# A hybrid four-layer model on one Trainium2 core: in the recurrent layer, other copies ahead of the triangular inverse, value rows moved by transfers, and two narrow products left whole

## The chip, the cores and the metric

The kernel runs on 1 core of one Trainium2 chip. The metric is the device time of one launch in microseconds (us). The kernel before was run three times: 2401.36, 2402.68 and 2403.2 us, median 2402.68 us. The profile is of one further execution.

## The reference, cut to what matters

Four layers, each a mixer and a gated feed-forward part, over 512 tokens of width 1024 in float32. The change lies in the first mixer alone, an RWKV-7 recurrence with 16 heads of 64:

```python
xx = token_shift(x) - x
xr, xw, xk, xv, xa, xg = (x + xx * mu[c] for c in range(6))
r, k, v = einsum('cbsd,cde->cbse', stack([xr, xk, xv]), w_rkv)
w = -softplus(-(w0 + tanh(xw @ w1) @ w2)) - 0.5      # w1: 1024 x 64
a = sigmoid(a0 + (xa @ a1) @ a2)                     # a1: 1024 x 64
g = sigmoid(xg @ g1) @ g2
kk = hs(k * k_k)
kk = kk * rsqrt(maximum(sum(kk * kk, -1), 1e-24))    # a sum over each head
k = k * (1 + (a - 1) * k_a)
def step(state, r_t, d_t, k_t, v_t, kk_t, a_t):      # 512 steps, state 64 x 64 per head
    sa = einsum('bhvk,bhk->bhv', state, kk_t)
    state = state * d_t - sa * (kk_t * a_t) + v_t * k_t
    return state, einsum('bhvk,bhk->bhv', state, r_t)
```

After it come the group norm of the outcome, the gate and the product with w_o.

## The kernel before, in words

**How the work is ordered.** The program records every operation, and a scheduler of its own writes each engine's order before the build (`Program.run`). All recorded operations therefore carry line 239 in the profile, and groups are told apart by tile names. The generators of the recurrence are interleaved by strings of letters and digits (`FIRST`, `PAIRED`, `ORDERS`, lines 28 to 34); the scheduler then moves operations within a window. Where it foresees that TensorE (PE) would stand idle it adds products of the identity (`keep_warm`, line 525), called fills here.

**Full products** split each float32 operand into a rounded part and the rest, both float32r, and take three float32r products for one (`mm3`). A split costs a cast on ScalarE (ACT) and a subtraction on VectorE (DVE): tiles `slot` for activations, `whi` and `wlo` for weights, read from `wraw`.

**The recurrent mixer** (`rwkv`, line 1009) works in these steps.
1. The k projection, then `heads`: the sum of squares of each head, by a product of the squared rows `t` with a 0/1 matrix of 16 columns (`selr`), 8 row tiles in split halves, so 16 products.
2. The r projection in 8 blocks of 24 products. Between them stand three narrow products (`lora`): w1 and a1 with 64 columns each (48 products in all, in split halves), and g1 with 128. `mixed` blends a row tile with its shifted one (DVE, tile `t`) and splits it. The results of w1 and a1 are the two halves of `twa`.
3. The v projection (`values`, tiles `v`), interleaved by `FIRST` with `ahead` (decays and scaled keys of a group of four heads, `rwkv_prepare`) and with the first `solve`.
4. For each of four groups of four heads, `solve`: `rwkv_products` masks 64-token blocks of key products into the tile `pr` or `pa`; `rwkv_inverse` inverts their triangles; `rwkv_direct` applies the inverses to the keys. The inverse first brings the 16x16 blocks on the diagonals together: eight ACT copies of 32 rows and 256 elements into `zx` (tiles `slot` or `et`), one DVE transpose, one addition. Then a loop of 15 steps on DVE, two operations a step, a second transpose, and two levels of products (`invert`, tiles `mt`, `low`, `iv`), whose two halves alternate by `PAIRED`.
5. `rwkv_chain` (line 1416) runs through the 8 chunks of 64 tokens of a group in turn, two chunks to a block b. Each chunk takes the state `st`, makes `vu` and makes the next state. A `vu` tile has 64 rows of v, copied from `v` by ACT (`vu<-v`, line 1445), and 64 rows of results from PSUM (`vu<-ps`); the pool holds four such tiles, two blocks. `ORDERS[n]` interleaves the chain of group n (c) with the outcome `rwkv_out` (o) and with the `solve` of group n+1 (p).
6. `rwkv_out_proj` multiplies by w_o (`et,rk`) beside the last chains, and the feed-forward part follows.

The few lines of `rwkv_inverse` that the change replaces:

```python
for k in range(4):
    r, o = slice(k * 32, k * 32 + 32), k % 2 * 32 + (P if k < 2 else 64)
    nc.scalar.copy(turn(zx4[r, :, 0, :]), turn(z3[r, o:o + 16, :]))
    nc.scalar.activation(turn(zx4[r, :, 1, :]), turn(z3[r, o + 16:o + 32, :]), AF.Identity, scale=mk['odd'][r])
nc.vector.transpose(n, zx)
nc.vector.tensor_add(n1, n2[:, :, 0, :], n2[:, :, 1, :])
```

Of the kernel before, what the change touches and what calls it, by code (L numbers as in the profile page):

```python
# [17 lines left out]
P = 128  # L18
S = 512
D = 1024  # L20
KT = D // P
HID = 2816
HT = HID // P
NB = S // P
# [482 lines left out]
class K:  # L507
# [509 lines left out]
    def rwkv(self, g, g_next, slots):  # L1017
# [5 lines left out]
        nc, d = self.nc, self.d  # L1023
# [6 lines left out]
        lp = self.pool("lp", 2, inner)  # L1030
        keep, sel, selr, rs = one("keep"), one("sel", w=46), one("selr", F32R, 30), one("kkrs", w=NB * 16)
        self.weight_pools(2, 2, wide, side="right")
# [10 lines left out]
        nc.vector.memset(sel[64:, 15:16], 1.0)  # L1043
        nc.vector.tensor_copy(selr, sel[:, :30])
        near, rbc = self.rstd(ms)
        xx = []

        def mixed(c, k):
            t = tp.tile([P, S], F32, name="t")
            x = xp.tile([P, S], F32R, name="slot"), xp.tile([P, S], F32R, name="slot")  # L1050
            nc.vector.scalar_tensor_tensor(t, xx[k], v['rw_mu'](c * KT + k), hn[k], op0=ALU.mult, op1=ALU.add)
            self.split(t, *x)
# [32 lines left out]
        for n in range(KT):  # L1085
            sq = tp.tile([P, S], F32, name="t")
            nc.scalar.activation(sq, kf[n], AF.Square, scale=v['rw_k_k'](n))
            part = [xp.tile([P, S], F32R, name="slot") for _ in range(2)]
            self.split(sq, *part)
            for j, t in enumerate(part):  # L1090
                nc.tensor.matmul(heads[:16], selr[:, 14 - 2 * n:30 - 2 * n], t, start=n + j == 0, stop=n == KT - 1 and j == 1)
        x = [mixed(0, k) for k in range(KT)]
        for n in range(KT):
            self.gemm(d['rw_w_r'][n], x, lambda ps: nc.scalar.copy(rf[n], ps))
            if n == 1:
                hs = tp.tile([P, S], F32, name="t")
                nc.scalar.copy(hs[:16], heads[:16])
                ps = self.bank()
                for b in range(NB):
                    nc.tensor.transpose(ps[:, b * 16:(b + 1) * 16], hs[:16, b * P:(b + 1) * P], self.ident[:16, :16])  # L1100
                hc = self.sm.tile([P, NB * 16], F32, name="kkss")
                nc.vector.tensor_scalar(hc, ps[:, :NB * 16], 1e-24, None, op0=ALU.max)
# [10 lines left out]
        cp = self.pool("cp", 1, early)  # L1113
        mk = cp.tile([P, 7 * 64 + 1], F32, name="mk")
        nc.sync.dma_start(mk, d['rw_masks'])
# [118 lines left out]
    def rwkv_prepare(self, sb, rf, kf, twa, keep, sel, rs, ka1):  # L1234
# [18 lines left out]
        for i, p in enumerate(sb['pairs']):  # L1253
# [13 lines left out]
            nc.scalar.activation(ei, sw, AF.Exp, scale=DEC)  # L1267
            nc.scalar.copy(wide.rearrange("p (b h d) -> p b h d", b=NB, h=2), rs3[:, :, 2 * p:2 * p + 2].unsqueeze(3).to_broadcast([P, NB, 2, 64]))
            nc.vector.tensor_copy(pend[:, i, :], self.blocks(e, NC)[:, :, C - 1])
# [45 lines left out]
    def rwkv_inverse(self, sb):  # L1315
# [4 lines left out]
        col = lambda j: slice(j * P, (j + 1) * P)  # L1320
        zx = self.part("et")
        zx4 = zx.rearrange("p (t x u) -> p t x u", t=16, x=2)
        z = sb['pr']
        z3 = z.rearrange("p (u t) -> p t u", u=16)
        for k in range(4):
            r, o = slice(k * 32, k * 32 + 32), k % 2 * 32 + (P if k < 2 else 64)
            turn = lambda t: t.rearrange("p t u -> p u t")
            nc.scalar.copy(turn(zx4[r, :, 0, :]), turn(z3[r, o:o + 16, :]))
            nc.scalar.activation(turn(zx4[r, :, 1, :]), turn(z3[r, o + 16:o + 32, :]), AF.Identity, scale=mk['odd'][r])
        n, tt, tmp = self.part("et"), self.part("et"), self.part("et")  # L1330
        nc.sync.dma_start(tt, self.d['rw_eye'])
        nc.vector.transpose(n, zx)
        n2, t4 = n.rearrange("p (t b m) -> p t b m", t=16, b=2), tt.rearrange("p (j b i) -> p b j i", j=16, b=2)
        n1 = zx[:, :256].rearrange("p (t m) -> p t m", t=16)
        nc.vector.tensor_add(n1, n2[:, :, 0, :], n2[:, :, 1, :])
        for i in range(1, 16):
# [69 lines left out]
    def rwkv_chain(self, sb, tg):  # L1406
# [11 lines left out]
        for b in range(NB):  # L1418
# [21 lines left out]
            for c, (rv, ru) in enumerate(halves):  # L1440
# [556 lines left out]
def consts():  # L1997
    import numpy as np
    i = np.arange(P)
    freq = (10000.0 ** (-2.0 * (i % 32) / 64)).astype(np.float32).reshape(P, 1)  # L2000
    s, t = i[:, None], i[None, :]
    s6, t6 = s % 64, t % 64
    even, odd = np.where(t < 64, s6 <= t6, s6 < t6), np.where(t < 64, s6 < t6, s6 <= t6)
    c = t[:, :64]
    low = [(s6 // (2 * m) == c // (2 * m)) & (s6 % (2 * m) >= m) & (c % (2 * m) < m) for m in (16, 32)]
    masks = [even, odd] + low + [s6 // 16 == c // 16, (s % 32 >= 16)]
# [19 lines left out]
def arrays(inputs):  # L2026
# [32 lines left out]
    a['rw_w_r'], a['rw_w_k'], a['rw_w_v'] = groups(rkv[0]), np.ascontiguousarray(rkv[1]), np.ascontiguousarray(rkv[2])  # L2059
    for n, m in (('rw_w1', 64), ('rw_a1', 64), ('rw_g1', P)):  # L2060
        a[n] = groups(a[n][0], m)[0]
    a['sw_w_qkv'] = groups(a['sw_w_qkv'][0])
# [77 lines left out]
```

## Time and profile before

| | |
|---|---|
| Three runs | 2401.36 to 2403.2 us, median 2402.68 us |
| Profiled execution | 2403.21 us, of which the span is 2401.4 us |
| Share of the span busy | PE 98%, DVE 81%, ACT 60%, POOL 14% |
| Recurrent mixer | from the start to some 420 us |
| Mean granted clock of PE | 0.997 of full speed |

How to read it: times inside the span count from its start. Two engines' work lies side by side, so a saving counts only where that engine is what the others wait for. PE's matmuls overlap each other in the records: one shown with 0.39 us can follow the last after 0.23 us, so PE's pace is taken from starts, not from durations. A float32 product stands as two records, a float32r one as one. "ACT" in the chain of waits means that the step was held by an ACT operation. In this kernel PE loads weights under PEld.

### The profile page before, as it was taken

What the parts mean: (1) busy time and instruction counts of PE and PEld (TensorE: products, weight loads), DVE (VectorE), ACT (ScalarE), POOL (GpSimd) and SP (SyncE); (2) the same over time, 40 slices, a digit from 0 to 9 for tenths busy, and PEclk for the clock granted to TensorE, in tenths of its full rate; (3) what the DMA queues carried; (4) which work ended last, traced back from release to release, by engine and by line L of the source; (5) the groups of instructions that cost most, each with busy time, mean ns of one, the idle gap of its engine ahead of it and who ended that gap; (6) DMA issues with size and microseconds to landing.
All of it is one profiled execution on the core that took longest, in us unless ns stands there. A gap on an engine that the chain in (4) does not pass through costs nothing.

```text
span 2401.4 us, 37056 instructions
## 1 busy us (share of the span) xinstructions
PE 2356.2 (98%) x13692; PEld 1939.1 (81%) x13692; DVE 1944.5 (81%) x3280; ACT 1450.9 (60%) x2540; POOL 328.1 (14%) x398
## 2 busy tenths in 40 slices
PE   9999889999999999999999999999999999999998
PEld 8577779988888768888887888888888778988886
DVE  8778986886879787868699888886869978886868
ACT  4666765755556587555575444755557747755555
POOL 0000000221121001211211100121111101121110
PEclk9999999999999999999999999999999999999999
DMA  4220012899998326999988754899898757899985
GB/s 160 84 77 13 9 66 72 193 209 229 219 212 206 89 72 140 212 230 227 212 216 208 196 152 104 183 217 222 220 219 207 171 138 168 203 204 232 219 209 117
DMA packets 129285, 404.27 MB, mean 168 GB/s; under 512 B 14416, under 2 KB 21072, under 8 KB 129104
## 3 DMA queue, kind: packets, MB, share of 16 engines
q0 software_dynamic: 51840, 176.18, 40.9%
q1 hardware_dynamic: 77264, 225.72, 28.1%
q8 instruction: 108, 1.77, 0.3%
q14 instruction: 73, 0.60, 0.1%
HBM read 397.39 MB, written 2.10 MB: 166 GB/s over the span
## 4 chain that ended last, share of the span: by engine, by line
PE 79%; DVE 7%; ACT 6%; DMA 4%; issue 4%; POOL 0%; SPq 0%; DVEq 0%; ACTq 0%; POOLq 0%
PE ps L239 78%; DMA wraw<-ffn_w_b 3%; DVE slot L239 2%; ACT slot L239 2%; DVE wlo L239 2%; ACT whi L239 1%; ACT et L239 1%; DMA wraw<-ffn_w_a 1%; DMA wraw<-ffn_o_b 0%; ACT vu L239 0%; DVE left L239 0%; DMA wraw<-sg_w_o 0%; ACT wu L239 0%; ACT L239 0%; DVE h L239 0%
## 5 line engine op out<-in xcount | busy, mean ns | idle before, releaser
L239 PE MATMUL ps<-whi,slot 128*128 128x512 f32 (+1 forms) x5072 | 1553.9, 384 | 4.8 <-DVE slot L239 4.2
L239 PEld LDWEIGHTS ps<-whi,slot 128*128 128x128 f32 x5072 | 943.5, 188 | 179.9 <-ACT whi L239 9.1
L239 ACT CAST whi<-wraw 128x1024 fp32r<-128x1024 f32 (+3 forms) x845 | 689.4, 836 | 563.1 <-PE ps L239 437.7
L239 DVE TENSOR_TENSOR wlo<-wraw,whi 128x1024 fp32r<-128x1024 f32 (+3 forms) x845 | 792.9, 955 | 244.9 <-ACT whi L239 243.3
L239 PE MATMUL ps<-wlo,slot 128*128 128x512 f32 (+1 forms) x2536 | 969.2, 383 | 3.1 <-DVE wlo L239 3.1
L239 PEld LDWEIGHTS ps<-wlo,slot 128*128 128x128 f32 x2536 | 476.6, 188 | 87.6 <-DVE wlo L239 7.4
L239 PE MATMUL ps<-slot,whi 128*128 128x512 f32 (+1 forms) x720 | 229.8, 396 | 2.0 <-ACT slot L239 1.3
L239 DVE TENSOR_TENSOR slot<-ps,slot 128x512 f32<-128x512 f32 (+2 forms) x271 | 161.3, 609 | 47.1 <-PE ps L239 32.9
L239 ACT CAST slot<-left 128x512 fp32r<-128x512 f32 (+1 forms) x294 | 164.8, 590 | 53.3 <-PE ps L239 29.4
L239 DVE TENSOR_TENSOR slot<-left,slot 128x512 fp32r<-128x512 f32 (+1 forms) x294 | 184.0, 647 | 11.0 <-ACT slot L239 6.9
L239 DVE TENSOR_TENSOR h<-h,ps 128x512 f32<-128x512 f32 x240 | 160.0, 685 | 27.9 <-PE ps L239 25.2
L239 POOL DMA_DIRECT2D wraw<-ffn_w_a x128 | 110.0, 863 | 500.5 <-DVE wlo L239 404.6
L239 PEld LDWEIGHTS ps<-slot,whi 128*128 128x128 f32 (+1 forms) x720 | 131.7, 186 | 40.0 <-DVE slot L239 7.9
L239 PE MATMUL ps<-slot,wlo 128*128 128x512 f32 (+1 forms) x360 | 140.3, 392 | 0.4 <-DVE wlo L239 0.4
L239 POOL DMA_DIRECT2D wraw<-ffn_w_b x64 | 55.0, 867 | 423.0 <-DVE wlo L239 156.3
L239 ACT COPY slot<-ps 128x512 f32<-128x512 f32 (+1 forms) x144 | 78.6, 563 | 36.7 <-PE ps L239 34.5
L239 POOL DMA_DIRECT2D wraw<-ffn_o_a x64 | 54.7, 855 | 285.3 <-DVE wlo L239 157.4
L239 ACT COPY left<-ps 128x512 f32<-128x512 f32 x108 | 54.9, 558 | 57.2 <-PE ps L239 57.2
L239 PE MATMUL ps<-ident,slot 128*128 128x128 f32 x561 | 86.2, 277 | 1.3 <-ACT slot L239 0.6
L239 PEld LDWEIGHTS ps<-ident,slot 128*128 128x128 f32 x561 | 63.3, 141 | 26.6 <-DVE slot L239 12.1
L239 PEld LDWEIGHTS ps<-slot,wlo 128*128 128x128 f32 (+1 forms) x360 | 66.7, 185 | 15.2 <-DVE wlo L239 1.2
L239 DVE SCALAR_TENSOR_TENSOR slot<-slot,ncol 128x512 f32<-128x512 f32 (+1 forms) x96 | 65.1, 702 | 9.2 <-ACT slot L239 9.0
(301 smaller groups left out, 2095.5 us busy)
## 6 DMA issues: line engine op xcount, KB each, us to landing
wraw<-ffn_w_a SPq DMA_DIRECT2D x128, 512.0 KB, 6.8
wraw<-ffn_w_a POOLq DMA_DIRECT2D x128, 512.0 KB, 7.0
wraw<-ffn_o_a SPq DMA_DIRECT2D x64, 512.0 KB, 5.1
wraw<-ffn_o_a POOLq DMA_DIRECT2D x64, 512.0 KB, 7.1
wraw<-ffn_w_b SPq DMA_DIRECT2D x64, 384.0 KB, 4.0
wraw<-ffn_w_b POOLq DMA_DIRECT2D x64, 384.0 KB, 6.3
wraw<-gla_w_p SPq DMA_DIRECT2D x24, 512.0 KB, 5.5
wraw<-gla_w_p POOLq DMA_DIRECT2D x24, 512.0 KB, 6.6
```

Of the source, the lines that this page charges most:

```text
L239: op = self.add(eng.name, lambda: getattr(eng.target, what)(*map(real, args), **{k: real(a) for k, a in kw.items()}), *self.price(eng.name ...
```

## The change

- **heads**: the squares are no longer split. One float32 product for each row tile, with 32 columns of `sel`, in four places of 32 rows of the bank: 8 products instead of 16. The four transposes after it take 128 rows.
- **w1 and a1**: their weights come as one array, are not split, and `blend` is not split. 16 float32 products of 64 columns, alternating between the upper and lower half of one bank, instead of 48. `tp` keeps three buffers for `t`.
- **solve**: the copies take 64 rows and 512 elements, four instead of eight, into two tiles. Each tile is transposed by DVE, and three operations with masks as per-row factors put them together, instead of one transpose and one addition.
- **chain**: the 64 rows of v come into `vu` by a transfer issued from GpSimd's queue (POOL), 32 in all, instead of an ACT copy.
- **order**: other strings for `FIRST`, `PAIRED` and `ORDERS[3]`, and whatever the scheduler makes of them. After the mixer the engines' orders are as before.

```diff
-ORDERS = "ffppcpqcpqqcopcopcoo", "ppcpqcpqqcopcopcoo", "ppcpcpcopcopcoo", "ccoccoc"
+ORDERS = "ffppcpqcpqqcopcopcoo", "ppcpqcpqqcopcopcoo", "ppcpcpcopcopcoo", "cccococ"
-FIRST = "vv0000vv0001v00vvv"
-PAIRED = "00110110010101"
+FIRST = "0v00v0v001vv00vv0v"
+PAIRED = "00011101110010"
...
-            part = [xp.tile([P, S], F32R, name="slot") for _ in range(2)]
-            self.split(sq, *part)
-            for j, t in enumerate(part):
-                nc.tensor.matmul(heads[:16], selr[:, 14 - 2 * n:30 - 2 * n], t, start=n + j == 0, stop=n == KT - 1 and j == 1)
+            o = n // 4 * 2
+            nc.tensor.matmul(heads[n % 4 * 32:n % 4 * 32 + 32], sel[:, 14 - o:46 - o], sq, start=n < 4, stop=n >= 4)
...
-                lora(1, d['rw_w1'], 64, twa[:64], AF.Tanh)
-            if n == 2:
-                lora(4, d['rw_a1'], 64, twa[64:], AF.Identity)
+                raw, ps = self.wr.tile([P, 1024], F32, name="wraw"), self.bank()
+                nc.sync.dma_start(raw, d['rw_wa1'])
+                for k in range(KT):
+                    for j, c in enumerate((1, 4)):
+                        r = slice(j * 64, j * 64 + 64)
+                        nc.tensor.matmul(ps[r], raw[:, k * P + j * 64:k * P + j * 64 + 64], blend(c, k), start=k == 0, stop=k == KT - 1, skip_group_check=True)
+                nc.scalar.activation(twa[:64], ps[:64], AF.Tanh)
+                nc.scalar.activation(twa[64:], ps[64:], AF.Identity)
...
+        z5 = z.rearrange("p (u g x t) -> p g u x t", u=16, g=8, x=2)
+        zx, zn = [self.part("et") for _ in range(2)], [self.part("et") for _ in range(2)]
+        for k in range(2):
+            for r, g in ((slice(0, 64), 4 + k), (slice(64, P), 2 + k)):
+                nc.scalar.copy(zx[k][r].rearrange("p (t x u) -> p u x t", t=16, x=2), z5[r, g])
+            nc.vector.transpose(zn[k], zx[k])
...
+        for (k, b), c, rest in (((0, 0), 0, n2(0, 1)), ((1, 0), 1, n1), ((1, 1), 2, n1)):
+            nc.vector.scalar_tensor_tensor(n1, n2(k, b), mk['odd'][:, c:c + 1], rest, op0=ALU.mult, op1=ALU.add)
...
-                nc.scalar.copy(vu[rv], sb['v'][b][rv])
+                nc.gpsimd.dma_start(vu[rv], sb['v'][b][rv])
```

**PE, the narrow products.** Before, a piece of the stretch in which heads (`selr`), w1 (64 columns) and the r projection (128 columns) stand mixed:

```order
L239 MATMUL ps<-slot,whi 128x512 x2
L239 MATMUL ps<-slot,wlo 128x512
L239 MATMUL ps<-slot,selr 16x512
L239 MATMUL ps<-slot,whi 64x512
L239 MATMUL ps<-slot,wlo 64x512
L239 MATMUL ps<-slot,selr 16x512
```

Now the same work stands together, heads as `sel` and both narrow products as `wraw`:

```order
L239 MATMUL ps<-t,sel 32x512
L239 MATMUL ps<-t,wraw 64x512 x3
L239 MATMUL ps<-t,sel 32x512
L239 MATMUL ps<-t,wraw 64x512 x2
L239 MATMUL ps<-t,sel 32x512 x2
```

The piece goes on in the same way to 23 narrow products with none of the r projection between them; the last `sel` follows four products later.

**PE, the first solve.** Before, the v projection (`whi,slot`, `wlo,slot`) ends ahead of the products of the first inverse (`pa`, `low`, `iv`), and fills (L525) stand among these:

```order
L239 MATMUL ps<-whi,slot 128x512
L239 MATMUL ps<-ew,sel 32x128 x4
L239 MATMUL ps<-h 128x128 x12
L239 MATMUL ps<-slot,pa 64x64 x13
L525 MATMUL ps<-ident 128x128 x3
L239 MATMUL ps<-slot,pa 64x64
L525 MATMUL ps<-ident 128x128
L239 MATMUL ps<-slot,pa 64x64 x18
```

Now the v projection's last products stand between them, and the 12 products of the next group (`h`) stand behind:

```order
L239 MATMUL ps<-slot,pa 64x64 x32
L239 MATMUL ps<-wlo,slot 128x512
L239 MATMUL ps<-slot,low 64x64 x16
L239 MATMUL ps<-slot,low 64x64 x16
L239 MATMUL ps<-whi,slot 128x512 x2
L239 MATMUL ps<-wlo,slot 128x512
L239 MATMUL ps<-whi,slot 128x512 x2
L239 MATMUL ps<-wlo,slot 128x512
L239 MATMUL ps<-slot,pa 64x64 x32
```

**ACT, the copies of the second solve** (from `pr` into `et`), before and now; `wu` and `vu` belong to the running chain:

```order
L239 COPY et<-pr 32x16x16 x2
L239 ACTIVATE et<-pr,mk 32x16x16 x2
L239 COPY et<-pr 32x16x16 x2
L239 ACTIVATE et<-pr,mk 32x16x16 x2
L239 COPY tok<-ps 128x512
```

```order
L239 COPY et<-pr 64x16x2x16
L239 ACTIVATE wu<-st,pend 128x128 x2
L239 COPY et<-pr 64x16x2x16
L239 COPY vu<-ps 64x256
L239 COPY et<-pr 64x16x2x16 x2
```

Eight copies without a break have become four with three operations of the chain among them.

## Rows read from the trace of the kernel before

**Rows 1.** The page: busy time of PE, and the chain that ended last by engine.

```profile
PE 2356.2 (98%) x13692; PEld 1939.1 (81%) x13692; DVE 1944.5 (81%) x3280; ACT 1450.9 (60%) x2540; POOL 328.1 (14%) x398
...
PE 79%; DVE 7%; ACT 6%; DMA 4%; issue 4%; POOL 0%; SPq 0%; DVEq 0%; ACTq 0%; POOLq 0%
```

**Rows 2.** Stretches: us, engines' busy us (records), PE clock, DMA share, GB/s.

```profile
62.08:95.30 33.22, 32.16 (x130) 18.48 (x129) 25.82 (x45) 22.58 (x39) 0.00 (x0) 1.00 0.21 72
...
194.19:210.81 16.62, 15.63 (x374) 14.19 (x373) 10.24 (x17) 4.58 (x13) 2.36 (x4) 1.00 0.02 7
210.81:253.00 42.19, 37.71 (x446) 25.91 (x446) 38.84 (x99) 38.20 (x79) 0.00 (x0) 0.92 0.04 11
...
353.00:388.00 35.00, 34.74 (x609) 31.16 (x611) 23.86 (x56) 21.12 (x54) 0.00 (x0) 1.00 0.13 40
```

**Rows 3.** PE in order of time: start, us, operation, records.

```profile
125.43 0.39 PE L239 MATMUL ps<-slot,wlo 128*128 128x512 f32 x1
...
132.23 0.39 PE L239 MATMUL ps<-slot,wlo 128*128 128x512 f32 x1
```

**Rows 4.** PE in order of time: float32 products.

```profile
95.30 1.12 PE L239 MATMUL ps<-twa,wa 64*128 64x512 f32 x2
...
159.90 0.43 PE L239 MATMUL ps<-ew,sel 128*32 128x128 f32 x8
...
166.64 1.89 PE L239 MATMUL ps<-twa,wa 64*128 64x512 f32 x8
```

**Rows 5.** Groups by form, 60 to 420 us: count, busy us, mean ns, idle before.

```profile
L239 DVE TENSOR_TENSOR slot<-t,slot 128x512 fp32r<-128x512 f32 x39 | 26.4, 690 | 15.8 <-PE ps L239 11.1 <-ACT slot L239 3.7
...
L239 ACT CAST slot<-t 128x512 fp32r<-128x512 f32 x39 | 22.6, 620 | 8.6 <-PE ps L239 8.2 <-DVE t L239 0.2
L239 DVE SCALAR_TENSOR_TENSOR t<-xx,vec,h 128x512 f32<-128x512 f32 x29 | 21.3, 750 | 0.6
...
L239 ACT COPY vu<-v 64x256 f32<-64x256 f32 x32 | 12.9, 402 | 0.3
...
L239 ACT ACTIVATE et<-pr,mk 32x256 f32<-32x256 f32 x8 | 5.9, 738 | 0.1
...
L239 ACT COPY et<-pr 32x256 f32<-32x256 f32 x8 | 5.1, 638 | 0.1
```

**Rows 6.** Fills alone (line 525) in a stretch: PE and PEld busy, clock.

```profile
194.19:210.81 16.62, 2.23 (x12) 1.64 (x12) 1.00 0.02 7
```

**Rows 7.** ACT and DVE around the copies of three solves, in order of time.

```profile
224.21 1.29 ACT L239 COPY et<-pr 32x256 f32<-32x256 f32 x2
...
231.62 0.40 DVE L239 TENSOR_TENSOR et<-et 128x256 f32<-128x256 f32 x1
...
286.75 0.71 DVE L239 STREAM_TRANSPOSE et<-et 128x512 f32<-128x512 f32 x1 [1.37 <-ACT et L239]
...
334.79 0.71 DVE L239 STREAM_TRANSPOSE et<-et 128x512 f32<-128x512 f32 x1 [1.99 <-ACT et L239]
```

**Rows 8.** The chain of waits, 210 to 353 us: first and last of seven `vu<-v` pieces.

```profile
238.32 0.40 ACT vu L239
...
341.60 0.40 ACT vu L239
```

**Rows 9.** PE in order of time, last chain: last read of block 0's `vu`, first of block 2's.

```profile
379.27 0.64 PE L239 MATMUL ps<-vu,pr 128*64 128x64 f32 x16
...
387.93 0.45 PE L239 MATMUL ps<-vu,tok 128*64 128x64 f32 x8 [0.19 <-ACT vu L239]
```

**Rows 10.** DMA issues: queue, count, KB each, median us to landing.

```profile
wraw<-ffn_w_a POOLq DMA_DIRECT2D x128, 512.0 KB, 7.0
...
slot<-slot SPq DMA_DIRECT2D x36, 64.0 KB, 2.0
...
h<-sg_b_o POOLq DMA_DIRECT2D x4, 512.0 KB, 12.0
```

**Rows 11.** A stretch of the first chain, as in rows 2.

```profile
232.00:236.00 4.00, 4.00 (x53) 3.30 (x52) 2.87 (x13) 3.96 (x11) 0.00 (x0) 0.50 0.00 0
```

More of the change, by code (lines that the diff above doesn't have):

```diff
@@ L1030, in rwkv @@
         lp = self.pool("lp", 2, inner)
-        keep, sel, selr, rs = one("keep"), one("sel", w=46), one("selr", F32R, 30), one("kkrs", w=NB * 16)
+        keep, sel, rs = one("keep"), one("sel", w=46), one("kkrs", w=NB * 16)
         self.weight_pools(2, 2, wide, side="right")
@@ L1043, in rwkv, with blend @@
         nc.vector.memset(sel[64:, 15:16], 1.0)
-        nc.vector.tensor_copy(selr, sel[:, :30])
         near, rbc = self.rstd(ms)
         xx = []
+        def blend(c, k):
+            t = tp.tile([P, S], F32, name="t")
+            nc.vector.scalar_tensor_tensor(t, xx[k], v['rw_mu'](c * KT + k), hn[k], op0=ALU.mult, op1=ALU.add)
+            return t
         def mixed(c, k):
-            t = tp.tile([P, S], F32, name="t")
             x = xp.tile([P, S], F32R, name="slot"), xp.tile([P, S], F32R, name="slot")
-            nc.vector.scalar_tensor_tensor(t, xx[k], v['rw_mu'](c * KT + k), hn[k], op0=ALU.mult, op1=ALU.add)
-            self.split(t, *x)
+            self.split(blend(c, k), *x)
             return x
@@ L1113, in rwkv @@
         cp = self.pool("cp", 1, early)
-        mk = cp.tile([P, 7 * 64 + 1], F32, name="mk")
+        mk = cp.tile([P, 7 * 64 + 3], F32, name="mk")
         nc.sync.dma_start(mk, d['rw_masks'])
@@ L1267, in rwkv_prepare @@
             nc.scalar.activation(ei, sw, AF.Exp, scale=DEC)
-            nc.scalar.copy(wide.rearrange("p (b h d) -> p b h d", b=NB, h=2), rs3[:, :, 2 * p:2 * p + 2].unsqueeze(3).to_broadcast([P, NB, 2, 64]))
+            nc.scalar.copy(wide.rearrange("p (b h d) -> p b h d", b=NB, h=2), rs3[:, :, p % 4 * 4 + p // 4 * 2:p % 4 * 4 + p // 4 * 2 + 2].unsqueeze(3).to_broadcast([P, NB, 2, 64]))
             nc.vector.tensor_copy(pend[:, i, :], self.blocks(e, NC)[:, :, C - 1])
@@ L1320, in rwkv_inverse @@
         col = lambda j: slice(j * P, (j + 1) * P)
-        zx = self.part("et")
-        zx4 = zx.rearrange("p (t x u) -> p t x u", t=16, x=2)
         z = sb['pr']
[L1324 to L1330, printed above, removed]
-        nc.sync.dma_start(tt, self.d['rw_eye'])
[L1332 to L1335, printed above, removed]
+        z5 = z.rearrange("p (u g x t) -> p g u x t", u=16, g=8, x=2)
+        zx, zn = [self.part("et") for _ in range(2)], [self.part("et") for _ in range(2)]
+        tt, tmp = self.part("et"), self.part("et")
+        nc.sync.dma_start(tt, self.d['rw_eye'])
+        for k in range(2):
+            for r, g in ((slice(0, 64), 4 + k), (slice(64, P), 2 + k)):
+                nc.scalar.copy(zx[k][r].rearrange("p (t x u) -> p u x t", t=16, x=2), z5[r, g])
+            nc.vector.transpose(zn[k], zx[k])
+        n, t4 = zn[0], tt.rearrange("p (j b i) -> p b j i", j=16, b=2)
+        n1 = zx[0][:, :256].rearrange("p (t m) -> p t m", t=16)
+        n2 = lambda k, b: zn[k].rearrange("p (t b m) -> p t b m", t=16, b=2)[:, :, b, :]
+        for (k, b), c, rest in (((0, 0), 0, n2(0, 1)), ((1, 0), 1, n1), ((1, 1), 2, n1)):
+            nc.vector.scalar_tensor_tensor(n1, n2(k, b), mk['odd'][:, c:c + 1], rest, op0=ALU.mult, op1=ALU.add)
         for i in range(1, 16):
@@ L2005, in consts @@
     low = [(s6 // (2 * m) == c // (2 * m)) & (s6 % (2 * m) >= m) & (c % (2 * m) < m) for m in (16, 32)]
-    masks = [even, odd] + low + [s6 // 16 == c // 16, (s % 32 >= 16)]
+    masks = [even, odd] + low + [s6 // 16 == c // 16, s % 32 < 16, (s % 64 >= 32) & (s % 32 < 16), s % 64 >= 32]
     masks = np.concatenate([m.astype(np.float32) for m in masks], axis=1)
@@ L2059, in arrays @@
     a['rw_w_r'], a['rw_w_k'], a['rw_w_v'] = groups(rkv[0]), np.ascontiguousarray(rkv[1]), np.ascontiguousarray(rkv[2])
-    for n, m in (('rw_w1', 64), ('rw_a1', 64), ('rw_g1', P)):
-        a[n] = groups(a[n][0], m)[0]
+    a['rw_g1'] = groups(a['rw_g1'][0])[0]
+    a['rw_wa1'] = groups(np.concatenate([a.pop('rw_w1')[0], a.pop('rw_a1')[0]], 1))[0]
     a['sw_w_qkv'] = groups(a['sw_w_qkv'][0])
```

6 lines of the change are left out of this document (3 added, 3 removed).

## Prediction

> **What bounds the kernel now.** I read the page first. PE is busy for 98% of the span and makes up 79% of the chain that ended last [rows 1]. For the whole program that says "PE-bound", but the change lies in the first 420 us only, and the engines' orders behind that are the same in both kernels. So the question is by how much the recurrent mixer ends earlier; what follows is dense product work that moves forward as one block.
>
> Next I read the stretches [rows 2]. From 62.08 to 95.30 us PE looks full (32.16 of 33.22 us), yet busy time of overlapping matmuls is not pace. The pace comes from starts: from 125.43 to 132.23 us lie 30 dense products [rows 3], so one takes 6.80 / 30 = 0.227 us. The 130 records of the stretch are then worth 29.5 us, and 3.7 us are lost waiting for split operands, while ACT casts for 0.62 us and DVE subtracts for 0.69 us a tile [rows 5].
>
> From 194.19 to 210.81 us the first inverse runs alone on PE. 0.99 us are idle and 2.23 us are fills [rows 6], 3.2 us together.
>
> From 210.81 us the chains run, and there PE's share says little, since its products are small and wait. In the first chain DVE works 38.84 and ACT 38.20 of 42.19 us [rows 2]. The timeline shows how they alternate: before each inverse stand eight gathering copies on ACT without a break, then DVE's transpose, which in two of three solves had waited 1.37 and 1.99 us for ACT [rows 7]. These copies are on the path. From 353 us PE has the output projection to fill every gap (34.74 of 35.00 us [rows 2]), so a wait less there is worth nothing.
>
> **The change, part by part.**
>
> *Narrow products on PE.* Removed: 48 + 16 = 64 products at 0.227 = 14.5 us. Added: 24 float32 products of 512 columns, a form that the trace shows only in relatives. One such product with full columns and half the rows stands with 1.12 us, four that alternate between two halves with 1.89 us, so a pair of halves shares 0.945 us; four places of 32 columns also share one time (0.43 us for four of 128 columns) [rows 4]. Perfect packing needs 8 pairs and 2 fours, 10 x 0.945 = 9.5 us; none at all 24 x 1.12 = 26.9 us. I take the printed order: runs of 3, 2, 3, 3, 3 and 2 wide products between runs of `sel`. These are 10 turns for the wide ones and 7 for `sel`, 17 x 0.945 = 16.1 us. Each of 12 changes of width adds half of 1.12 - 0.945, 0.09 us: 1.1 us. Sum 17.2 us, 2.7 us more than before.
> The Trainium skill (TensorEngine Tiling (Array Packing), Key Properties) says that tiles of one configuration run in parallel, but that changing the configuration drains the engine. Rows 4 agree on the first; no row has the two widths side by side. By the first alone the sum would be the 9.5 us above, with the second it is near my 17.2.
>
> *ACT and DVE in that stretch* lose 24 casts of 0.62 us and 24 subtractions of 0.69 us [rows 5]. What remains for DVE, 16 blends of 0.75 us or 12.0 us [rows 5], is less than PE's 17.2 us, so PE no longer waits and the 3.7 us go. If the three `t` buffers couple them too closely, PE waits again; that is inside the upper bound of 26.9 us.
>
> *First inverse.* The order now puts the v projection's last products between its phases and no fill. I count the 3.2 us as gone. The group products (`h`) that move behind it cost nothing, as the masking on DVE that reads them takes longer. Front in all: +2.7 - 3.7 - 3.2 = -4.2 us.
>
> *Gathering copies.* Eight at 0.638 and 0.738 us are 5.5 us a solve [rows 5], as in the piece from 224.21 us [rows 7]. Four copies of 512 elements: a straight one of that length takes 0.62 us [rows 5], and two of the old strided ones 1.28 us. I take 0.75, nearer to the first, since 64 rows by 256 straight cost 0.402 us [rows 5] against 0.638 for 32 rows by 256 strided, and part of that difference must be paid once an instruction. So 3.0 us, 2.5 saved. Behind the last copy DVE now does a transpose and two mask operations, 0.71 + 2 x 0.46, instead of 0.71 + 0.40 [rows 7] (0.46 is 0.40 plus the 0.06 by which the blend exceeds a subtraction [rows 5]): +0.5 us. Net -2.0 us, in three solves -6.0 us; the first solve's copies lie under the v projection.
>
> *DVE's other additions*, a transpose and one mask operation, 1.2 us a solve, fall into the waits of 1.37 and 1.99 us [rows 7] in two solves. In the other DVE had none: +1.2 us.
>
> *Rows of v.* 32 ACT copies of 0.402 us go [rows 5]. Seven of them lie on the chain of waits ahead of 353 us, 2.6 us together, the first at 238.32 and the last at 341.60 us [rows 8]: -2.6 us. The later ones have PE's filling work beside them. The transfers in their place are hidden if they land in time: block 0's `vu` is last read by 379.9 us, and block 2's first reader starts at 387.93 [rows 9], so 8.0 us. A transfer of 64 KB lands after 2.0 us from SP's queue, one of 512 KB after 7.0 from POOL's [rows 10]. I take them as hidden; queued ahead of them on POOL are only the small `out` products, which the order puts early.
>
> **Sum:** -4.2 - 6.0 + 1.2 - 2.6 = -11.6 us. The profiled execution took 2403.2 us, so 2391.6; it stands 0.5 us above the median of the runs, so **2391 us**. A measurement can tell about 0.2% from no change, 4.8 us.
>
> **The rivals.**
>
> *More than that.* The two widths pack side by side (9.5 us, 7.7 less), the copies run at 0.62 us (3 x 4 x 0.13 = 1.6 less), and the stretch from 232 to 236 us, in which PE ran at half clock (0.50) [rows 11] behind the eight copies, is back at full, worth 2.0: 11.3 us less, **2380 us**. For it: tiles do run side by side in rows 4. Against: widths alternate.
>
> *DVE is the bound of the chains.* At 38.84 of 42.19 us [rows 2] it may be what ends every step; ACT's saved time was then cover. The copies give nothing, three solves add 0.71 + 3 x 0.46 - 0.40 = 1.7 us each, 5.1, and -4.2 - 2.6 + 5.1 = -1.7 us: **2401 us**. For it: DVE had no wait in the first chain's solve. Against: its waits of 1.37 and 1.99 us in the next two.
>
> *The narrow products run one by one*, 26.9 instead of 17.2 us: **2401 us**. For it: float32 and three buffers; against: rows 4.
>
> *Slower: the transfers land late.* POOL's queue also shows 12.0 us to landing [rows 10]. Against a window of 8.0 us each block that waits for a buffer would lose 4.0 us, six of them in the last three chains 24 us: **2415 us**. It decides from a landing of 8.0 us on. Against it: those transfers were eight times as large, from DRAM, and added in flight.
> The Trainium skill (SBUF — State Buffer, SBUF: two separate sides) has a rule that speaks for this rival: a transfer from GpSimd's queue stalls while DVE holds the shared port, because its descriptors can't be written. No run here shows that yet.
>
> **How the numbers follow.** The forecast has 0.60; its own range is 2384 to 2398, the upper end from copies at 1.28 us. More: 0.10. DVE the bound: 0.12. One by one: 0.08. Late transfers: 0.10. The first two are faster by over 0.2%: 0.70. The next two are within it: 0.20. Slower: 0.10. From 2379 to 2402 us the range takes in all but the late transfers and the edges of the others.
>
> **What would show it.** In the profile after: the narrow products take 15 to 19 us from the first `sel` to the last `wraw`, with no split tiles of heads and w1 left on DVE; no fills between the phases of the first inverse; gathering copies of 64 rows at 0.65 to 0.85 us, and DVE's first loop step 2 us earlier behind the masks; the first chain 6 us earlier or more, the output projection's end 10 to 13 us earlier; `vu` transfers landing in 2 to 4 us with no PE wait put down to them. It is wrong if the strided copies take over 1.2 us, if the narrow stretch exceeds 25 us, or if `vu` products wait for DMA.

## The result, and the profile after

The changed kernel takes 2412.03 us (median of 6 runs, 2408.74 to 2412.81), the kernel before beside it 2403.08 us (2401.36 to 2404.08): ratio 1.0036, 95% interval 1.0026 to 1.0045. It is slower by 8.7 us, where 11.6 us less were forecast. Below, a ratio is turned into us by 2403: 0.001 is 2.4 us.

The page of the changed kernel, as in [rows 1]:

```profile
PE 2364.1 (98%) x13678; PEld 1941.9 (81%) x13678; DVE 1936.2 (80%) x3265; ACT 1421.2 (59%) x2466; POOL 344.1 (14%) x430
...
PE 83%; DVE 8%; ACT 4%; DMA 3%; issue 1%; SPq 0%; POOL 0%; DVEq 0%; ACTq 0%; POOLq 0%
```

ACT lost 29.7 us of work and 74 instructions, yet the span went from 2401.4 to 2409.7 us. As the order behind the mixer is the same, I followed the mixer. PE in order of time, at the places that the prediction spoke of (start, us, operation, records, and in brackets the wait and what ended it):

```profile
68.23 1.05 PE L239 MATMUL ps<-t,sel 128*32 128x512 f32 x2
...
83.85 1.08 PE L239 MATMUL ps<-t,wraw 128*64 128x512 f32 x4
...
85.98 1.04 PE L239 MATMUL ps<-t,sel 128*32 128x512 f32 x2
...
133.67 0.39 PE L239 MATMUL ps<-slot,wlo 128*128 128x512 f32 x1
...
170.17 0.66 PE L239 MATMUL ps<-ident,slot 128*128 128x128 f32 x4 [2.03 <-ACT slot L239]
...
206.62 1.16 PE L239 MATMUL ps<-iv,slot 64*64 64x64 f32 x64
...
220.64 0.45 PE L239 MATMUL ps<-vu,tok 128*64 128x64 f32 x6
...
275.39 1.16 PE L239 MATMUL ps<-rk 64*128 64x128 f32 x8 [0.84 <-ACT h L239]
278.07 2.21 PE L239 MATMUL ps<-rk 64*128 64x128 f32 x12 [1.52 <-DVE grs L239]
282.08 0.69 PE L239 MATMUL ps<-vu,tok 128*64 128x64 f32 x8
...
405.46 0.69 PE L239 MATMUL ps<-vu,pr 128*64 128x64 f32 x16
```

The same places in the kernel before:

```profile
136.31 0.39 PE L239 MATMUL ps<-slot,wlo 128*128 128x512 f32 x1
...
208.51 1.28 PE L239 MATMUL ps<-iv,slot 64*64 64x64 f32 x48 [0.47 <-DVE iv L239]
...
216.56 0.45 PE L239 MATMUL ps<-vu,tok 128*64 128x64 f32 x8
...
397.55 0.69 PE L239 MATMUL ps<-vu,pr 128*64 128x64 f32 x16
```

The r projection ends at 134.06 us instead of 136.70. The first inverse's last products end at 207.78 instead of 209.79, so the front brings 2.0 us. From there to the first chain's first `vu` product the changed kernel takes 12.9 us instead of 6.8, so this product starts 4.1 us later than before. The chains lose more: the last product of the last chain starts at 405.46 us, 7.9 us later than before (397.55). New are a wait of 2.03 us for ACT at 168 us and a stretch at half clock from 277 us on. Stretches, with columns as in [rows 2]:

```profile
62.08:95.30 33.22, 33.22 (x118) 15.45 (x117) 19.97 (x30) 13.09 (x20) 0.00 (x0) 1.00 0.16 52
...
207.80:282.10 74.30, 63.72 (x972) 50.38 (x968) 68.18 (x161) 51.03 (x100) 10.84 (x19) 0.96 0.10 26
...
276.00:292.00 16.00, 14.36 (x119) 11.78 (x120) 12.70 (x34) 6.73 (x12) 0.00 (x0) 0.57 0.07 17
```

From 276 to 292 us the granted clock is 0.57, where before it was 1.00. The dip of [rows 11] is gone and a longer one has come. Over the whole mixer, before and now:

```profile
60.00:420.00 360.00, 338.89 (x3954) 267.04 (x3954) 288.03 (x667) 232.56 (x460) 13.19 (x24) 0.99 0.16 53
```

```profile
60.00:420.00 360.00, 337.57 (x3873) 261.13 (x3872) 278.09 (x648) 199.69 (x385) 30.27 (x56) 0.97 0.18 55
```

Summed over stretches of 4 us, PE stands at half clock for some 7 us before and for some 20 us now. At half clock at most half of such a time is lost. By this estimate up to 7 of the 8.7 us can be the clock's. The falls at 171 and 277 us come with the waits of 2.03 and 1.52 us above, so the clock follows waits here, but what a wait costs and what the clock adds are not told apart.

Groups by form from 60 to 420 us, the changed kernel, which answer to [rows 5]:

```profile
L239 ACT COPY et<-pr 64x512 f32<-64x512 f32 x8 | 8.6, 1080 | 0.1
L239 DVE TENSOR_TENSOR rk<-out,rk 128x256 fp32r<-128x256 f32 x15 | 8.4, 596 | 1.8 <-ACT rk L239 1.8
...
L239 ACT COPY slot<-pa 64x512 f32<-64x512 f32 x4 | 4.6, 1147 | 1.1 <-DVE pa L239 1.0
L239 ACT COPY et<-pa 64x512 f32<-64x512 f32 x4 | 4.4, 1088 | 0.0
```

A gathering copy takes 1.08 to 1.15 us, not 0.75. The program's scheduler, too, has another figure: its price for an ACT copy is `95.0 + n * 0.833` ns, 0.52 us for 512 elements, with nothing for the pattern. For a tile of 32 rows it adds 200 ns, which made 0.51 us of the old copies that took 0.64 [rows 5]. Four copies a solve now last 2.2 us longer than the order allows for; the old eight were off by about half of that.

ACT in the first and second solve of the changed kernel:

```profile
163.74 4.63 ACT L239 COPY slot<-pa 64x512 f32<-64x512 f32 x4 [1.02 <-DVE pa L239]
168.40 1.07 ACT L239 COPY v<-ps 128x512 f32<-128x512 f32 x2
169.50 0.62 ACT L239 COPY slot<-kkrs 128x512 f32<-128x512 f32 x1
...
224.90 1.06 ACT L239 COPY et<-pr 64x512 f32<-64x512 f32 x1
225.98 0.36 ACT L239 COPY vu<-ps 64x256 f32<-64x256 f32 x1
226.37 2.17 ACT L239 COPY et<-pr 64x512 f32<-64x512 f32 x2
228.57 0.37 ACT L239 COPY wu<-ps 128x256 f32<-128x256 f32 x1
```

In the first solve 4.63 us of copies stand ahead of `slot<-kkrs`, for which PE's transposes wait at 168 us. In the second the copies stand between the small copies of the running chain (`vu<-ps`, `wu<-ps`).

DVE and GpSimd (POOL) at 270 us:

```profile
269.96 2.70 DVE L239 TENSOR_TENSOR rk<-out,rk 128x256 fp32r<-128x256 f32 x1
```

```profile
268.99 1.05 POOL L239 DMA_DIRECT2D vu<-v  x2 [16.45 <-ACT out L239]
270.05 2.32 POOL L239 TENSOR_TENSOR out<-v,bonus 128x256 f32<-128x256 f32 x4
```

The pair of `vu` transfers had waited 16.45 us at the head of GpSimd's queue, with the `out` products behind it. The profile names an ACT operation on `out` as the end of the wait; that the pair waited for its buffers, of which the pool holds four, is read from the order. Then four products run together, and DVE's product, usually 0.4 us, takes 2.70. The same long product stands in the profile of every run below that leaves GpSimd's queue as it is here (e3, e5, e6, e7, e11, e13), and in none of the others.

### The profile page after: what moved, and what is told of

The parts are those of the page before. It is cut to its first block, busy times and chain, and to the rows that moved or that the text cites. A ratio compares the mean times of both kernels' runs of the same rounds, so it can differ in the third digit from the quotient of the medians.

```text
span 2409.7 us, 37014 instructions
## 1 busy us (share of the span) xinstructions
PE 2364.1 (98%) x13678; PEld 1941.9 (81%) x13678; DVE 1936.2 (80%) x3265; ACT 1421.2 (59%) x2466; POOL 344.1 (14%) x430
## 3 DMA queue, kind: packets, MB, share of 16 engines
q8 instruction: 107, 1.75, 0.3%
## 4 chain that ended last, share of the span: by engine, by line
PE 83%; DVE 8%; ACT 4%; DMA 3%; issue 1%; SPq 0%; POOL 0%; DVEq 0%; ACTq 0%; POOLq 0%
PE ps L239 82%; DMA wraw<-ffn_w_b 3%; DVE slot L239 2%; ACT slot L239 2%; DVE wlo L239 2%; PE ps L525 1%; ACT whi L239 1%; DVE ew L239 1%; ACT et L239 1%; DVE et L239 1%; DVE qk L239 0%; DVE h L239 0%; DVE left L239 0%; DMA wraw<-ffn_o_a 0%; DVE rk L239 0%
## 5 line engine op out<-in xcount | busy, mean ns | idle before, releaser
L239 PE MATMUL ps<-slot,whi 128*128 128x512 f32 x688 | 217.0, 395 | 1.0 <-ACT slot L239 1.0
L239 PEld LDWEIGHTS ps<-slot,whi 128*128 128x128 f32 x688 | 127.7, 188 | 32.7 <-DVE slot L239 2.6
L239 PE MATMUL ps<-slot,wlo 128*128 128x512 f32 x344 | 133.9, 391 | 0.0
L239 PEld LDWEIGHTS ps<-ident,slot 128*128 128x128 f32 x561 | 63.2, 141 | 27.9 <-DVE slot L239 12.7
L239 PEld LDWEIGHTS ps<-slot,wlo 128*128 128x128 f32 x344 | 64.6, 188 | 14.2 <-DVE wlo L239 0.8
```

The lines of the kernel that those rows point to most:

```text
L239: op = self.add(eng.name, lambda: getattr(eng.target, what)(*map(real, args), **{k: real(a) for k, a in kw.items()}), *self.price(eng.name ...
```

## The experiments

The expectations give a number for each theory. In the runs marked "order held" the operation is recorded as it was, so that the scheduler writes the same order for every engine, and only what is emitted in its place differs.

**e1: v rows from SyncE's queue** (changed kernel, order held)

```diff
                 nc.gpsimd.dma_start(vu[rv], sb['v'][b][rv])
+                nc.ops[-1].call = lambda a=vu[rv], s=sb['v'][b][rv]: nc.sync.target.dma_start(a.real(), s.real())
```

> The changed kernel with every engine's order held, but the 32 transfers of v rows go out on SyncE's queue instead of GpSimd's. Theory 1 (GpSimd's queue): its four products come in one run at 270 us because transfers that wait for a buffer stand ahead of them, and DVE's product beside them takes 2.70 us instead of 0.4; PE then idles and falls to half clock from 276 to 292 us. Without the transfers in that queue 2.3 us of DVE and about 3.5 us of half clock go: some 5.8 us less than the changed kernel, 2406. Theory 2 (order): DVE stands full from 270 to 286 us because eight masking products are ahead of the chain's first state; that stays, so at most 1 us less, 2411, and the clock still falls to 0.50. Theory 3 (transfers land late): no wait of PE is put down to a transfer, so no change.

Measured: 1.0022 (1.0011 to 1.0032), 3.4 us under the changed kernel's ratio. DVE and GpSimd in this run:

```profile
272.65 0.75 DVE L239 TENSOR_TENSOR rk<-out,rk 128x256 fp32r<-128x256 f32 x2
```

```profile
261.04 1.19 POOL L239 TENSOR_TENSOR out<-v,bonus 128x256 f32<-128x256 f32 x2 [52.74 <-DVE gvar L239]
...
268.16 2.04 POOL L239 TENSOR_TENSOR out<-v,bonus 128x256 f32<-128x256 f32 x2 [5.94 <-DVE iv L239]
```

The products come in two pairs, DVE's product is back at 0.38 us, and the clock from 276 to 292 us is 0.89. Some 6 us were expected; about half came. The profile is of the slowest of e1's eight runs (2410.82 us): PE stands in it at half clock for some 24 us of the mixer, in other places, so it shows the products apart but not what that is worth.

**e2: v rows by ACT again** (changed kernel, order held; `nc.scalar.target.copy` in the same place)

> The changed kernel with every engine's order held, but the v rows are copied by ACT again, at the place of the transfers. Theory 1: as in the run with SyncE's queue 5.8 us go, while up to seven copies of 0.4 us lie on the chains again: 2406 to 2409. Theory 2: the order stays, 2412 to 2415.

Measured: 1.0045 (1.0028 to 1.0061). Theory 1 missed: in this order the 32 copies cost at least as much as the transfers in GpSimd's queue; whether more is inside the intervals. Against e1, the run with the transfers elsewhere, they cost 0.0023 or 5.5 us.

**e3: the last two copies of the first solve later** (changed kernel; the emission of two copies and of what depends on them is put off until four copies of `v` and one of `kkrs` are out)

```diff
-            op.call()
+            self.emit(op)
...
+    HOLD, late = {949: 1047, 950: 1047}, []
+    def emit(self, op):
+        if op.i in self.HOLD or any(d in self.late for d in op.deps):
+            self.late.append(op)
+            return
...
```

> The changed kernel, in which the last two of the four gathering copies of the first solve stand behind four copies of v and one of kkrs on ACT; nothing else is moved but what depends on them. Theory 1 (the wide copies take 1.08 to 1.16 us instead of some 0.75, and four in a row hold ACT for 4.6 us): PE's wait of 2.03 us at 168 us and the dip of the clock behind it go, the first inverse ends 2 to 4 us earlier than 207.8, and the kernel is 2 to 4 us faster, 2408 to 2410. Theory 2 (DVE's loop sets the end of the first inverse): its transposes come 2.3 us later, the inverse ends where it did, no change.

Measured: 1.0028 (1.0018 to 1.0038). PE's wait at 168 us is gone and the first inverse ends 2.8 us earlier:

```profile
203.78 1.16 PE L239 MATMUL ps<-iv,slot 64*64 64x64 f32 x64
...
281.67 0.69 PE L239 MATMUL ps<-vu,tok 128*64 128x64 f32 x8
```

But the first `vu` product of the second chain starts at 281.67, 0.4 us earlier than in the changed kernel. What the first solve's end gains is mostly used up by then. In this profile the clock is 0.50 from 232 to 236 us, where the changed kernel's is 1.00, so a part of that may be the clock.

**e4: GpSimd's products ahead of the waiting pair** (changed kernel, the same `emit` with `HOLD = {2238: 2599, 2252: 2599}`)

> The changed kernel, in which the four GpSimd products at 270 us stand ahead of the pair of transfers that waits there for its buffers; all else held. Theory 1: they run as soon as their operands are there, earlier and not in one run beside DVE's product, so the 2.70 us shrink and the half clock behind them too: 2 to 6 us less, 2406 to 2410. If their operands come no earlier, they stand as four in a row again and nothing changes. Theory 2: no change in either case.

Measured: 1.0023 (1.0013 to 1.0033), the same as e1 although the transfers are still GpSimd's. The products come in two pairs here too, and DVE's are short again:

```profile
271.09 0.75 DVE L239 TENSOR_TENSOR rk<-out,rk 128x256 fp32r<-128x256 f32 x2
```

So it is the place in the queue that costs, not the queue that issues them. Each of the two intervals by itself reaches close to the changed kernel's; that e9 and e14 show the same cost again makes it firm.

**e5: less work on DVE** (changed kernel, order held)

```diff
             nc.vector.transpose(zn[k], zx[k])
+            if k:
+                nc.ops[-1].call = lambda: None
...
             nc.vector.scalar_tensor_tensor(n1, n2(k, b), ...)
+            if k:
+                nc.ops[-1].call = lambda: None
```

> The changed kernel, order held, with the second transpose and two of the three mask operations of each inverse left out (the inverses lose part of their diagonal blocks): 0.71 + 2 x 0.48 = 1.67 us of DVE less a solve. Theory A (DVE is the bound from 208 to 314 us, where it is busy for 94.8 of 106 us): the two solves there give 3.3 us, the third one up to 1.7 more; ratio to the kernel before some 1.0015 to 1.0022 instead of 1.0036. Theory B (ACT's copies are what the solves wait for): these operations fit into waits for ACT, at most 1 us less, ratio above 1.003.

Measured: 1.0035 (1.0021 to 1.0048), nothing. Theory A's 1.0015 to 1.0022 only touches the interval's lower end. A cost of DVE's additions under some 3 us could not be seen here.

**e6: straight copies** (changed kernel, order held)

```diff
                 nc.scalar.copy(zx[k][r].rearrange(...), z5[r, g])
+                nc.ops[-1].call = lambda a=zx[k][r], s=z[r, k * S:(k + 1) * S]: nc.scalar.target.copy(a.real(), s.real())
```

> The changed kernel, order held, but each gathering copy reads 512 adjacent elements of each row instead of the pattern (so the inverses work on other numbers): expected 0.62 us instead of 1.08 a copy, 1.84 us of ACT less a solve. Theory A: PE's wait of 2.03 us at 168 us goes and the first inverse ends 2 to 3 us earlier, but DVE gives it back before 280 us, as it did where the copies were moved: 2 us less at most, ratio 1.0028 or more. Theory B: 1.84 us in each of four solves, and the clock's dip at 172 us: 6 to 8 us less, ratio near 1.0005.

Measured: 1.0002 (0.9993 to 1.0011), 8.2 us less: theory B. By form, in this run:

```profile
L1334 ACT COPY et<-pr 64x512 f32<-64x512 f32 x8 | 4.9, 616 | 0.1
...
L1334 ACT COPY slot<-pa 64x512 f32<-64x512 f32 x4 | 2.5, 618 | 0.0
L1334 ACT COPY et<-pa 64x512 f32<-64x512 f32 x4 | 2.5, 618 | 0.0
```

The sixteen copies shrink from 17.6 to 9.9 us, 7.7 us of ACT, and the kernel by 8.2. In this order the kernel loses as much as the copies last longer, the first solve's among them. PE's time at half clock falls as well, from some 20 to some 10 us, so not all of the 8.2 us need be time in which something waited for a copy.

**e7: e5 and e6 together** (order held)

> The changed kernel, order held, with both: straight copies, and without the second transpose and two mask operations. Theory A: as with less work on DVE alone, and up to 2 us more. Theory B: as with straight copies alone. If ACT and DVE are on the path in turn, both gains add up: 10 us or more, and the kernel is faster than the one before by 1 to 3 us.

Measured: 0.9998 (0.9989 to 1.0008). Less work on DVE adds 1.0 us, inside both intervals, which leave room for 3 us more or less. Together with e5 this speaks against theory A.

**e8: transfers from GpSimd in the order of before** (kernel before, order held)

```diff
                 nc.scalar.copy(vu[rv], sb['v'][b][rv])
+                nc.ops[-1].call = lambda a=vu[rv], s=sb['v'][b][rv]: nc.gpsimd.target.dma_start(a.real(), s.real())
```

> The kernel before, every engine's order held, with the 32 copies of v rows replaced by transfers from GpSimd's queue at the same places. As forecast in the prediction: seven copies of 0.4 us leave the chains, 2.6 us less, ratio 0.9989. Theory 1 (GpSimd's queue): its products stand behind transfers that wait for buffers, come in longer runs, and DVE stalls beside them for 1 to 3 us: ratio 0.9995 to 1.0010. If transfers land late, PE's waits for vu grow and the ratio is above 1.001.

Measured: 0.9999 (0.9989 to 1.0008). Neither a loss nor the 2.6 us of the forecast, which lie at the interval's edge: the transfers land in 1.9 us (median), and `rk<-out,rk` takes 0.45 us as before.

**e9: e1 and e6 together** (order held)

> The changed kernel, order held, with straight gathering copies (other numbers in the inverses) and the v rows from SyncE's queue: the two edits that gave 8.2 and 3.1 us alone. If the two costs are separate they add up: ratio 1.0036 - 0.0034 - 0.0014 = 0.9988. If both only remove the same half-clock stretch at 276 to 292 us, the second adds little: ratio 1.000.

Measured: 0.9983 (0.9974 to 0.9993). The two costs are separate and add up: 12.7 us under the changed kernel, 4.1 us under the one before. The clock is 1.00 from 276 to 292 us and in the whole mixer, so up to 10 of the 12.7 us can have come by way of the clock:

```profile
276.00:292.00 16.00, 14.44 (x238) 10.87 (x237) 15.45 (x48) 11.38 (x29) 0.00 (x0) 1.00 0.12 35
...
60.00:420.00 360.00, 344.23 (x3983) 268.49 (x3981) 282.95 (x665) 198.69 (x394) 13.97 (x24) 1.00 0.18 58
```

**e10: the copies' term alone** (kernel before, order held; of the eight copies of a solve two emit a straight one of 64 rows each for two halves, the others nothing)

```diff
+            q = slice(k * 32, k * 32 + 64)
             nc.scalar.copy(...)
+            nc.ops[-1].call = (lambda: None) if k % 2 else (lambda a=zx[q], s=z[q, :S]: nc.scalar.target.copy(a.real(), s.real()))
             nc.scalar.activation(...)
+            nc.ops[-1].call = lambda: None
```

> The kernel before, order held, with the eight gathering copies of 5.5 us a solve replaced by four straight ones of 0.62 us (2.5 us; the inverses work on other numbers). This is the term of my sum taken alone, and larger: ACT saves 3.0 us a solve. By the prediction's reading (ACT's copies are on the path in three solves) 6 to 9 us less, ratio 0.9963 to 0.9975. If DVE, 93% busy from 210 to 276 us, is the bound of that stretch, what ACT saves becomes waiting: at most 2 us less, ratio 0.999 to 1.000.

By the edit two copies a solve are left, not four (the expectation has it wrong), so ACT saves 5.5 - 1.2 = 4.3 us a solve. Measured: 0.9981 (0.9971 to 0.9991), 4.6 us. Three solves save ACT 12.9 us, and the kernel gets about a third of it. The copies are on the path in the order of before as well, but not for all they last.

**e11: the copies write adjacent elements** (changed kernel, order held; the same copy, walked as `"p t x u"`)

> The changed kernel, order held; each gathering copy walks the same elements in the other order, so that it writes adjacent ones and reads with the stride, where it now reads runs of 16 and writes with the stride. If the stride of the writes is what makes 1.08 us of 0.62, the copies come near 0.62 and the kernel near that with straight copies, ratio 1.0002. If the stride costs the same on the reading side, 1.08 us and a ratio of 1.0036 stay; if reading with a stride of 256 elements costs more, it gets slower.

Measured: 1.0043 (1.0029 to 1.0057); the copies take 1.08 to 1.13 us. Reading with this stride (256 elements) costs as much as writing with the other (32).

**e12: the narrow products alone** (no other part of the change, and strings for the order chosen for these operations by a search over the scheduler's own plans; those for the chains differ too)

```diff
-ORDERS = "ffppcpqcpqqcopcopcoo", "ppcpqcpqqcopcopcoo", "ppcpcpcopcopcoo", "ccoccoc"
+ORDERS = "ffppcpqcpqcqocppocoo", "ppcpqcpqqcopcopoco", "ppcpcpcopcopcoo", "ccoccco"
-FIRST = "vv0000vv0001v00vvv"
-PAIRED = "00110110010101"
+FIRST = "v00v0v00v0100vvvv0"
+PAIRED = "01001101010101"
...
```

> Only the part of the change with the narrow products (heads, w1 and a1 unsplit): the eight old copies, ACT's copies of v rows, and other strings for the order, chosen for these operations. If the loss came from copies that last twice what the order allows for and from transfers in GpSimd's queue, what the front saves (r projection's end 2.6 us earlier) can reach the end: 3 to 6 us faster than the kernel before, ratio 0.9975 to 0.9988. If DVE, full from the first inverse to the second chain, takes back whatever the front saves, the ratio is 0.9995 to 1.0005 whatever the order.

Measured: 0.9998 (0.9989 to 1.0007). The r projection ends at 134.29 us, the gain of the front is there, and it doesn't reach the end. In its profile (of the slowest of its runs, 2404.93 us) the first chain's first `vu` product starts 2.3 us earlier than before, at 214.24, and the last product of the last chain 0.9 us later, at 398.49. The clock is low in two stretches:

```profile
228.00:240.00 12.00, 11.15 (x132) 8.24 (x132) 9.48 (x36) 9.83 (x26) 0.00 (x0) 0.72 0.01 3
276.00:292.00 16.00, 12.50 (x159) 9.93 (x155) 12.57 (x34) 13.59 (x29) 0.00 (x0) 0.85 0.08 26
```

**e13 and e14: copies in runs, nothing left out** (changed kernel, order held; e14 has e1's edit besides)

```diff
                 nc.scalar.copy(...)
+                nc.ops[-1].call = lambda a=zx[k][r].rearrange('p (u x t) -> p u x t', u=16, x=2), s=z5[r, g]: nc.scalar.target.copy(a.real(), s.real())
             nc.vector.transpose(zn[k], zx[k])
+            nc.ops[-1].call = lambda a=zn[k].rearrange('p (t x u) -> p t x u', t=16, x=2), s=zx[k].rearrange('p (u x t) -> p t x u', u=16, x=2): nc.vector.target.transpose(a.real(), s.real())
```

> The changed kernel, order held; the gathering copies write in the order in which they read, in runs of 32 adjacent elements, and DVE's two transposes read with the stride instead. Theory B (ACT's copies set the solves, 1.84 us each, and DVE's additions cost nothing): the copies fall to 0.62 or 0.65 us; DVE's transposes may rise from 0.71 to some 1.1; ratio 1.0036 falls to 1.0002 to 1.0010. Theory A (DVE full from 208 to 314 us): what ACT saves DVE pays, 0.4 us a transpose, ratio 1.002 or more. If a run of 32 is no cheaper than the old pattern, 1.08 and 1.0036 stay.

> The same, and the v rows on SyncE's queue. If both costs are told apart rightly the ratio is that with straight copies and SyncE's queue, 0.9983, or up to 0.001 above it for DVE's longer transposes: 2 to 4 us faster than the kernel before with the reference's numbers. If DVE gives it back, 1.000 or more.

Measured: e13 1.0013 (1.0004 to 1.0022), e14 0.9987 (0.9978 to 0.9996), 2398.07 us beside 2401.54. By form, in e14 (L1336 are the two transposes of the gather):

```profile
L1336 DVE STREAM_TRANSPOSE et<-et 128x512 f32<-128x512 f32 x6 | 6.5, 1076 | 0.1
L1334 ACT COPY et<-pr 64x512 f32<-64x512 f32 x8 | 4.9, 616 | 0.1
...
L1334 ACT COPY et<-pa 64x512 f32<-64x512 f32 x4 | 2.5, 619 | 0.0
L1334 ACT COPY slot<-pa 64x512 f32<-64x512 f32 x4 | 2.5, 619 | 1.1 <-DVE pa L239 1.0
```

The copies fall to 0.62 us, DVE's transposes rise from 0.71 to 1.08, and of the 8.2 us that straight copies gave 5.5 are left. The 2.7 us between them may be DVE's, but lie inside the intervals. With the transfers out of GpSimd's queue, 6.2 us less (e14 against e13), this version is faster than both kernels, by 3.1 us than the one before.

## Why the prediction was wrong

**The step that failed: "I take 0.75, nearer to the first" for the gathering copies, and beside it that the sum counts each saving in full as time on the path.** The copies took 1.08 to 1.15 us. I had the upper end at 1.28, "two of the old strided ones", and the range's 2384 to 2398 went up to it, but as a term that only saves less: four copies of 1.08 are still 1.1 us a solve shorter than the eight. By the sum's own terms 1.08 instead of 0.75 takes 3.9 us in three solves and leaves -7.7, so the size alone does not turn the sign. What I left out is that an order written for a duration can turn an error of it into waiting. e6 shows the price: 8.2 us for 7.7 us of copies, nearly all of the 8.7. That the order was written for 0.52 us stands in the code; that this is why the copies bind more here than in e10 is argued, not shown, since no run had an order written for 1.08.

None of the prediction's three signs of being wrong came: the copies stayed under 1.2 us, the narrow stretch under 25, and no `vu` product waited for a transfer. It had no sign for a saving that nothing waited for.

**"The first solve's copies lie under the v projection": wrong.** The sum has them at nothing. They held ACT for 4.63 us, PE waited 2.03 us for a copy behind them, and the first inverse ended 2.8 us later than it could (e3).

**"Queued ahead of them on POOL are only the small `out` products": the wrong side of the queue.** What cost time was not what stood ahead of the transfers: the products stood behind them. The transfers land in 2.0 us (median), no wait of PE is put down to them, and the rival with late transfers did not come. The sign of that rival came from the same queue by another way: 3.4 us (e1) and 3.1 us (e4) alone, 4.6 us on top of straight copies (e9 against e6). The rule of the Trainium skill that spoke for it (SBUF — State Buffer, SBUF: two separate sides) says that such a transfer stalls while DVE runs in a mode that takes the shared port. No run here shows that: beside a DVE that is busy for 92% the transfers land in 2.0 us.

**The rows of v, -2.6 us: not seen.** In the order of before the replacement is worth 0.2 us (e8: 0.9999, give or take 2.3); in the new order the copies cost 5.5 us against SyncE's transfers (e2 against e1).

**DVE's additions, +1.2 us: not seen either** (e5, e7), though so little could hide in the intervals. The rival in which DVE is the bound had the right place, a full DVE, which is busy for 92% from 207.8 to 282.1 us, and the wrong price. A share of busy time alone does not say which instruction others wait for.

**The narrow products: right in size, in part by luck.** 17.2 us were worked out; 23 products take from 68.23 to 84.86, the last one 0.98 more, 17.6 us. But PE's turns hang on when the operands are made, as the prediction feared of the three `t` buffers. At 16 of the turns PE's weight load (PEld) had waited for a `t` from DVE or ACT; here for the third of the first three wide products and for the second of the two `sel` that stand together:

```profile
70.12 0.19 PEld L239 LDWEIGHTS ps<-t,wraw 128*64 128x64 f32 x2 [0.72 <-DVE t L239]
...
74.04 0.14 PEld L239 LDWEIGHTS ps<-t,sel 128*32 128x32 f32 x2 [0.74 <-ACT t L239]
```

These two `sel` take 1.86 us and share nothing, where the sum has one turn of 0.945 for them. So the trace does not tell a cost for the change of width from the wait for a buffer. The rule of the Trainium skill (TensorEngine Tiling (Array Packing), Key Properties) that a change of configuration drains the engine is neither borne out nor refuted by it. PE no longer waits for split operands, and the r projection ends 2.6 us earlier; -1.0 was forecast. What was removed had thus cost 20.2 us and not the 18.2 of the sum.

**The sum.** Forecast and result are 20.3 us apart. Without the two costs the kernel is 12.7 us faster (e9), and the rest of the change gives 4.1 us, where my sum with copies of 0.62 us would be 13.2. In e9's profile the first inverse ends 6.0 us earlier than before (203.82 against 209.79), more than the 4.2 forecast, and yet the first `vu` product of the first chain starts at 216.68, as before (216.56):

```profile
202.66 1.16 PE L239 MATMUL ps<-iv,slot 64*64 64x64 f32 x64
...
214.21 2.18 PE L239 MATMUL ps<-h 64*128 64x128 f32 x32
216.32 0.42 PE L239 MATMUL ps<-ew,sel 128*32 128x128 f32 x8
216.68 0.45 PE L239 MATMUL ps<-vu,tok 128*64 128x64 f32 x6
```

The moved group products (`h`) that I costed at nothing stand ahead of it now. They are not all lost: from the first chain's start to the second's e9 takes 3.4 us less than before.

The terms that were measured alone, each in an order of its own, are small too: 0.2 us for the rows of v (e8), 0.5 for the narrow products (e12), and of what ACT saves on the copies a third (e10), which is 3 of the 9 us that copies of 0.62 us save in three solves. Together that is 3.7 us, close to the 4.1. Each of them has an interval of some 2 us either way, so the agreement may be luck. It speaks for savings that nothing waited for as the place of the missing 9 us. How much of it is the new order and how much the chains' own waits stays open.

## What to carry to other kernels

A copy that gathers with a stride costs by its pattern, not by its elements: measure one of the new shape before the sum (here it was 1.75 to 1.85 times the straight one), and give the price to whatever plans the order. A saving counts only where something waits for it: take it in full only after one run with that term alone. A transfer that waits for a buffer at the head of a queue holds all that is queued behind it; what then comes in one run may meet another engine. An edit of durations in a kernel with a fixed order is judged with the order held, part by part, or the order's own effect is mixed in.

## What the hardware showed that was not expected

An ACT copy of 64x512 float32 takes 0.62 us when it reads and writes adjacent elements (e6), or reads in runs of 32 and writes in a row (e13), and 1.08 to 1.15 us when it writes with a step of 32 elements (the changed kernel) or reads with one of 256 (e11). DVE's transpose takes 1.08 us when it reads with a step of 32 (e13, e14) instead of 0.71. The Trainium skill (SBUF — State Buffer, Door 1: The DMA port swizzle) says that accesses within one line of 16 bytes run at full speed and each step to a new line pays; the direction of these numbers agrees.

One DVE product whose operands both lie in SBUF stood for 2.70 us instead of 0.4 beside four GpSimd products of 2.32 us together. The Trainium skill (SBUF — State Buffer, SBUF: two separate sides) says that such a DVE instruction and a GpSimd one that reads SBUF exclude each other, and that the one that starts first holds the shared pair for its whole instruction. The trace agrees that the two keep each other off and differs in how: DVE's product starts 0.09 us ahead of the first of the four, and yet outlasts all of them. That the 2.70 us are a wait for the ports is not shown; with GpSimd's products in pairs DVE's takes 0.38 us (e1, e4).

PE's clock falls to 0.50 at 277 us, within the second of two waits, 0.84 and 1.52 us, between small products. How much of the time PE has the full clock changes from run to run of one kernel: of e1's runs the fastest (2402.65 us) has a mean granted clock of 0.997, the slowest (2410.82) 0.994. The runs of the kernel before beside it lie between 2398.58 and 2403.43 us, all at 0.996 or 0.997.
